# One core, a hybrid decoder layer in three-pass float32: every operand tile of the wide matrix products moved to one start address modulo 512

## The chip, the core and the metric

The kernel runs on one core of a Trainium2 chip. The metric is the device time of one execution in microseconds, the median of several runs. One further execution was recorded by the hardware profiler; every duration below is from that one.

## What is computed

One layer on 16 learned meta tokens and 512 tokens of 1,024 channels. A forgetting-attention branch (8 heads of 128) and an mLSTM branch (4 heads, keys of 256, values of 512, chunks of 128 tokens) read the same normalised input `h`; gates merge them, and one output projection follows. Cut to what matters:

```python
h = rms_norm(x, g_pre)                  # 528 tokens x 1024
z = h @ w_in                            # 1024 x 14352, split into 13 parts
oa = forgetting_attention(fq, fk, fv, log_sigmoid(ff + b_fox_f))
ya = (oa * silu(fz)) @ w_a
qk = silu(causal_conv(mqk, conv_w, conv_b))
hb = sigmoid(mo) * mlstm_scan(mq, mk, mv, ...)
yb = (rms_norm(hb, g_head) * silu(mz)) @ w_b
merged = sigmoid(ga) * ya + sigmoid(gb) * yb
out = x + rms_norm(merged @ w_o, g_post)
```

## The kernel before

Every float32 operand is split into a high part (`..h`, float32r) and a low remainder (`..l`), and each product is made of three passes: high by high, high by low, low by high (`mm3`, lines 132 to 135). One pass is one TensorE instruction with 128 rows and up to 512 moving columns; ahead of each stands a load of its 128 x 128 stationary operand, which the profiler lists as an engine of its own (PEld). While one pass streams its moving operand, the stationary operand of the next is loaded.

Two forms of projection exist. In `proj_t` (line 137) the weights are stationary and 512 tokens of `hh`/`hl` stream; in `proj_wide` (line 160) 128 tokens of `hh`/`hl` are stationary and 512 weight columns stream. For `mo` and `mz` of the mLSTM branch, seven products per block take the place of eight (`st_products`, line 272): their operands are sums of token blocks (`t1` to `t4`, made once by `st_tokens`, line 189) and sums of weight blocks, 256 columns at a time. In `mo` (heads 1 to 3) the token sums are stationary and the weights stream; in `mz` it is the other way round. The order of work per mLSTM head is: transpose and gate the head before, queries and keys with their convolution (264 and 258 columns), `wb` product of the head before (`wb_part`, line 800), values, scores, `mo`, numerator, `mz`. Then come four pairs of attention heads, and last the gates `ga`, the product with `w_a`, and the output projection (`pout`). The instructions of an engine run in program order.

On-chip tiles come from pools. A pool lays its tags behind one another in the order in which they first come up, each as large as the largest tile that asks for it and as often as its `bufs` says, in steps of 64 bytes here; the pools stand behind one another in the order const, wts, work, mlstm, and fox takes the place of mlstm for the second half. 1,152 bytes per partition lie ahead of the first tile. So the start of each tile follows from the sizes, and with it what this text calls the *phase*: the byte address in the partition modulo 512. `hh` and `hl` hold 8 rows (one for each 128 channels) of 528 tokens, 2,112 bytes apart, so that the phase of token 16, where nearly all products begin, moves on by 64 from row to row.

| operand (lines) | phase before | phase after |
|---|---|---|
| `hh`, `hl` from token 16, rows 0 to 7 | 256, 320, 384, 448, 0, 64, 128, 192 | 64 in every row |
| `hm` (meta tokens) | 192 | 64 |
| weight tiles `raw`, `whi`, `wlo`, any block of 128 columns | 256 | 64 |
| `bh`, `bl`, `pth`, `ptl`, `gh1`, `gl1` (tags `big_h`, `big_l`) | 128 | 64 |
| `gh0`, `gl0`, attention values (tags `vh`, `vl`) | 384 | 64 |
| `mh0`, `ml0`; `mh1`, `ml1` (tags `qk0h` to `qk1l`) | 128; 384 and 128 | 64 |
| `mh2`, `ml2`, `mh3`, `ml3` (pool fox) | 320, 64, 320, 320 | 64 |
| token sums `t1` to `t4`, small weight blocks `whs`, `wls` | 320 | 0 |
| attention's meta values `vm` | 256 | 0 |

Of the kernel before, what the change touches and what calls it, by code (L numbers as in the profile page):

```python
# [8 lines left out]
F32 = mybir.dt.float32  # L9
F32R = mybir.dt.float32r  # L10
BF16 = mybir.dt.bfloat16
# [3 lines left out]
P = 128  # L15
DM = 1024
KC = DM // P
SEQ = 512
NM = 16
L = NM + SEQ  # L20
HL = L // 2
NCH = SEQ // P
# [19 lines left out]
OFFA = [0, 144, 416, 816]  # L42
NA = 1344

OFFP = [0, 256, 640, 1152]


@with_exitstack
def tile_hybrid_block(ctx: ExitStack, tc: tile.TileContext, x, meta, norm_pre, norm_post, w_in, b_fox_f,
# [7 lines left out]
    cp = ctx.enter_context(tc.tile_pool(name="const", bufs=1))  # L57
# [6 lines left out]
    def psum1(name):  # L64
        return pa.tile([P, 512], F32, tag="pa", name=name)

    def banks(name, n):

        return [psum1(f"{name}_{i}") for i in range(n)]

    def line(pool, name, n=1, parts=P, **kw):

        return pool.tile([parts, -(-n // 16) * 16], F32, name=name, **kw)[:, 0:n]


    ident = cp.tile([P, P], F32, name="ident")
    make_identity(nc, ident)
    mhalf = line(cp, "mhalf")
    G.memset(mhalf, -0.5)
    hh = cp.tile([P, KC, L], F32R, name="hh")  # L80
    hl = cp.tile([P, KC, L], F32R, name="hl")
    hm = cp.tile([P, KC, P], F32R, name="hm")
    yb = cp.tile([P, KC, SEQ], F32, name="yb")
    gc = cp.tile([P, 96], F32, name="gc")
# [2 lines left out]
    wk = ctx.enter_context(tc.tile_pool(name="work", bufs=1))  # L87
# [1 line left out]
    mw = c1.enter_context(tc.tile_pool(name="mlstm", bufs=1))  # L89

    def sb(shape, dt, tag, name, pool=None, **kw):
        return (pool or wk).tile(shape, dt, tag=tag, name=name, **kw)


    wsrc = sb([P, 512], BF16, "y", "wsrc", bufs=2)
# [20 lines left out]
    def wchunk(*args):  # L116

        return wsplit(wload(*args))
# [13 lines left out]
    def mm3(ps, ah, al, bh, bl, start, stop, **kw):  # L132
        T.matmul(ps, ah, bh, start=start, stop=False, **kw)  # L133
        T.matmul(ps, ah, bl, start=False, stop=False, **kw)  # L134
        T.matmul(ps, al, bh, start=False, stop=stop, **kw)  # L135
# [211 lines left out]
    def stat_part(b):  # L347
        xt, n = xs[b]
        junk = sb([P, 2, 512], BF16, "vh", f"junk{b}")
        ss = line(wk, f"ss{b}", 1, tag="ss", bufs=5)  # L350
        if b == 0:
            half = line(wk, "ss_half", 1, tag="rs", bufs=5)
            junk2 = sb([P, 512], BF16, "y", "junk_half", bufs=2)
            pin(S.activation(junk[:, 0, :], xt[:, 0, :], AF.Square, accum_out=half))
            pin(V.tensor_tensor_reduce(out=junk2, in0=xt[:, 1, :], in1=xt[:, 1, :], op0=ALU.mult, op1=ALU.add,
                                       scale=1.0, scalar=0.0, accum_out=ss))
            pin(V.tensor_tensor(ss, ss, half, ALU.add))
        else:
            pin(S.activation(junk[:n], xt, AF.Square, accum_out=ss[:n]))
        pin(V.tensor_scalar(ss[:n], ss[:n], 1.0 / DM, EPS, ALU.mult, ALU.add))  # L360
        rs = line(wk, f"rs{b}", 1, tag="rs", bufs=5)
        pin(G.tensor_tensor(rs[:n], ss[:n], mhalf[:n], ALU.pow))
        rstd.append(rs)

# [64 lines left out]
    def v_part(h):  # L429
        v = v_tiles(h)  # L430
        w = wchunk(win, 0, KC, C_MV + h * MV, MV, f"wv{h}")
        pn = banks(f"pv{h}", NCH)
        pm = psum1(f"pvm{h}")
        proj_wide(pn, w, pm)
        v_split(*v, pn, pm)
        return v
# [99 lines left out]
    vh, vl, vm = v0  # L536
# [49 lines left out]
    a = gi  # L586
# [137 lines left out]
    def mo_part(h):  # L724
        so = sb([P, NCH, MV], F32, "w", f"so{h}")
        pn = banks(f"po{h}", NCH)

        snaps = [so.rearrange("p s (m n) -> p m s n", m=2)[:, m] for m in range(2)]
        units = [(pn[m], pn[2 + m], snaps[m], slice(m * P, m * P + P)) for m in range(2)]
        st_products(st_wide(C_MO + h * MV, f"wo{h}"), units)  # L730

        dry = line(wk, f"dry{h}", 1, tag="ss", bufs=5)
        pin(S.activation(dry, mhalf, AF.Sigmoid))
        for i in (1, 0):
            for m in range(2):
                dst = so[:, :, i * 256:i * 256 + 256].rearrange("p (s m) n -> p m s n", m=2)[:, m]
                S.activation(dst, units[m][i].rearrange("p (s n) -> p s n", s=2), AF.Sigmoid)
        return so
# [13 lines left out]
    def value_part(h, wpk, v, so, hts, chunks):  # L752
        wh, wl = wpk
        vh, vl, vm = v
        for c in chunks:
            pn = (psum1(f"pna{h}{c}"), psum1(f"pnb{h}{c}"))
            for u in (1, 0):
                o, n = u * 256, 256 + 2 * u
                for j in range(c + 1):
                    s0 = OFF[j] + (c - j) * P  # L760
                    T.matmul(pn[u][:, 0:n], wh[:, s0:s0 + P], vh[:, j, o:o + n], start=(j == 0), stop=False)
                    T.matmul(pn[u][:, 0:256], wh[:, s0:s0 + P], vl[:, j, o:o + 256], start=False, stop=False)
                    T.matmul(pn[u][:, 0:n], wl[:, s0:s0 + P], vh[:, j, o:o + n], start=False, stop=False)
                T.matmul(pn[u][:, 0:n], wh[:, OFFM + c * P:OFFM + (c + 1) * P], vm[:, o:o + n],
                         start=False, stop=True)
            r = line(wk, f"r{h}{c}", 1, tag="r", bufs=4)
            V.tensor_scalar(r, pn[1][:, 256:257], -1.0, col[:, NB + NCH + c, 8 + h:9 + h], ALU.mult, ALU.max)
            V.tensor_tensor(r, pn[1][:, 256:257], r, ALU.max)
            V.reciprocal(r, r)
            if c % 2:  # L770
                ht2 = sb([P, 2, MV], F32, ("qk0h", "qk0l")[c // 2], f"ht{h}{c}")
            ht = ht2[:, c % 2, :]
            for u in range(2):
                V.scalar_tensor_tensor(ht[:, u * 256:u * 256 + 256], pn[u][:, 0:256], r,
                                       so[:, c, u * 256:u * 256 + 256], ALU.mult, ALU.mult)
            junk = sb([P, MV], BF16, "y", f"mjunk{h}{c}", bufs=2)
            ss = line(wk, f"mss{h}{c}", 1, tag="ss", bufs=5)
            S.activation(junk, ht, AF.Square, accum_out=ss)
            V.tensor_scalar(ss, ss, 1.0 / MV, EPS, ALU.mult, ALU.add)
            rs = line(wk, f"mrs{h}{c}", 1, tag="rs", bufs=5)  # L780
            G.tensor_tensor(rs, ss, mhalf, ALU.pow)
            V.tensor_scalar(ht, ht, rs, None, ALU.mult)
            hts[c] = ht
# [37 lines left out]
    for h in range(MH):  # L821
# [6 lines left out]
        if h:  # L828
            w = decay(h)
        if pend is not None:  # L830
            wb_part(pend[0], bt)
        if h == 0:
            v = v0
# [5 lines left out]
            w = decay(0)  # L839
        else:  # L840
            v = v_part(h)
# [74 lines left out]
    def prob_part(p, m, q, k):  # L916
# [7 lines left out]
        for c in range(NCH):  # L924
# [16 lines left out]
            V.reciprocal(rsum, rsum)  # L941
            o = OFFP[c]
            G.tensor_scalar(pn[:, o:o + P].rearrange("p (g t) -> p g t", g=4),  # L943
# [4 lines left out]
    def ptr_part(p, m, pn):  # L948
# [5 lines left out]
        for c in range(NCH):  # L954
            o = OFFP[c]
            pt = psum1(f"pt{h}{c}")
# [45 lines left out]
    q = fq_part(0)  # L1002
    c1.close()
    gp = ctx.enter_context(tc.tile_pool(name="fox", bufs=1))
    go = gp.tile([P, FH, SEQ], F32, tag="go", name="go")
    k = fk_part(0)
    wb_part(MH - 1, bt)
    for p in range(FH // 2):
# [5 lines left out]
        if p % 2 == 0:  # L1014
            v = fv_part(p)
# [46 lines left out]
        S.activation(mh_[u], sa, AF.Copy)  # L1062
        V.tensor_tensor(ml_[u], sa, f(mh_[u]), ALU.subtract)
    og = yb.rearrange("p (b u) t -> p b (u t)", b=NCH)
    oss = line(cp, "oss", NCH * 3).rearrange("p (b i) -> p b i", i=3)
    opre = line(cp, "opre", NCH)

    def out_end(ps, b, c0, n, i):
# [4 lines left out]
    w = wchunk(wo, 0, KC, 0, 512, "wo_0")  # L1073
# [8 lines left out]
    for u in (2, 3):  # L1082
        w = wchunk(wo, 0, KC, u * 256, 256, f"wo{u}")
        for b in range(NCH):
            ps = psum1(f"pout{u}{b}")
            for k in range(KC):
                mm3(ps[:, 0:256], mh_[k // 2][:, k % 2, b * P:(b + 1) * P], ml_[k // 2][:, k % 2, b * P:(b + 1) * P],
                    w[0](k, 0, 256), w[1](k, 0, 256), k == 0, k == KC - 1)
            out_end(ps[:, 0:256], b, u * 256, 256, u - 1)
            if u == 3:  # L1090
                rs = line(wk, f"ors{b}", 1, tag="rs", bufs=5)
                V.scalar_tensor_tensor(rs, oss[:, b, 2:3], 1.0 / DM, opre[:, b:b + 1], ALU.mult, ALU.add)
                G.tensor_tensor(rs, rs, mhalf, ALU.pow)
                for i in range(2):
                    cs = slice(i * 512, i * 512 + 512)
                    V.scalar_tensor_tensor(og[:, b, cs], og[:, b, cs], rs, xr[:, b, cs], ALU.mult, ALU.add)
                    nc.sync.dma_start(out2[b * P:(b + 1) * P, cs], og[:, b, cs])
            elif u == 2:
                V.tensor_reduce(opre[:, b:b + 1], oss[:, b, 0:2], axis=mybir.AxisListType.X, op=ALU.add)
                V.tensor_scalar(opre[:, b:b + 1], opre[:, b:b + 1], 1.0 / DM, EPS, ALU.mult, ALU.add)  # L1100
# [25 lines left out]
```

## Time and profile before

| | |
|---|---|
| median of 3 runs | 958.07 us (957.95 to 959.13) |
| the profiled execution | 959.97 us, of which the span from first to last instruction is 958.1 us |
| TensorE, products (PE) | 942.0 us busy, 98% of the span, 5,720 instructions |
| TensorE, stationary loads (PEld) | 835.7 us busy, 5,720 instructions |
| VectorE, ScalarE, GpSimd | 572.5, 439.7 and 140.4 us busy |
| granted TensorE clock, mean | 0.994 |

In all rows times are microseconds unless a column says ns; L134 is line 134 of the kernel before; `pyb<-bl,wb_h` names what is written and what is read, buffer numbers left out; `128x512` is the moving operand. A matrix product lasts from its start to the end of its last result, and the next one starts long before that, so the durations of neighbours overlap.

### The profile page before, as it was taken

To read this page: it belongs to the slowest core of one execution; us is meant where nothing else is said; L and a number is where in the kernel's file an instruction comes from. 1 tells how busy PE (TensorE), PEld (TensorE's weight loads), DVE (VectorE), ACT (ScalarE), POOL (GpSimd) and SP (SyncE) were. 2 spreads that over 40 slices of the span, in tenths; PEclk is the share of its full clock that TensorE was granted. 3 is DMA by queue.
4 is the path that set the end of the run, shared out by engine and by line. 5 is a ranking of instruction groups with operands and counts; after the bars stand their busy time and mean duration, and the time that the engine had idled before them with its cause. 6 is when DMAs were issued, how large, how long until landed. Compare 5 with 4: busy or idle time off the path is not lost.

```text
span 958.1 us, 14295 instructions
## 1 busy us (share of the span) xinstructions
PE 942.0 (98%) x5720; PEld 835.7 (87%) x5720; DVE 572.5 (60%) x966; ACT 439.7 (46%) x740; POOL 140.4 (15%) x186
## 2 busy tenths in 40 slices
PE   8999899999999999999999999999999999999997
PEld 6998799889998899988999888898888888888887
DVE  6998588448886288862788445445345454444443
ACT  5646446436565255562555224456235365423331
POOL 3054100122001220012112010123111012100000
PEclk9999899999999999999999999999999999999999
DMA  6222143303323223322224242323332322522302
GB/s 225 91 70 78 45 132 97 91 23 93 117 79 102 63 66 111 110 64 80 78 85 164 87 137 68 105 91 111 88 95 95 88 83 72 176 88 92 106 23 89
DMA packets 71469, 90.05 MB, mean 94 GB/s; under 512 B 4965, under 2 KB 56261, under 8 KB 71402
## 3 DMA queue, kind: packets, MB, share of 16 engines
q1 hardware_dynamic: 70344, 89.09, 30.4%
q8 instruction: 45, 0.74, 0.3%
q10 hardware_dynamic: 1058, 0.04, 0.1%
q14 instruction: 22, 0.18, 0.1%
HBM read 86.95 MB, written 2.16 MB: 93 GB/s over the span
## 4 chain that ended last, share of the span: by engine, by line
PE 90%; DVE 4%; ACT 2%; DMA 1%; issue 1%; POOL 1%; POOLq 0%; DVEq 0%; ACTq 0%; SPq 0%
PE pyb L133 3%; PE pyb L135 3%; PE pyb L134 3%; PE pz L134 3%; PE pz L133 3%; PE pz L135 3%; PE pqk L135 3%; PE pqk L133 3%; PE pv L133 3%; PE pv L135 3%; PE pqk L134 3%; PE pv L134 3%; PE po L134 2%; PE po L135 2%; PE po L133 2%; PE pfk L135 2%
## 5 line engine op out<-in xcount | busy, mean ns | idle before, releaser
L943 POOL TENSOR_SCALAR pn<-lt,rsum 128x128 f32<-128x128 f32 x32 | 23.1, 723 | 211.8 <-DVE rsum L941 211.8
L134 PE MATMUL pyb<-bl,wb_h 128*128 128x512 f32 x128 | 50.6, 395 | 0.0
L135 PE MATMUL pyb<-bh,wb_l 128*128 128x512 f32 x128 | 50.6, 395 | 0.0
L133 PE MATMUL pyb<-bh,wb_h 128*128 128x512 f32 x128 | 50.5, 395 | 0.0
L134 PE MATMUL pv<-wv_l,hh 128*128 128x512 f32 (+1 forms) x128 | 46.9, 366 | 1.5 <-DVE wv_l L127 1.5
L135 PE MATMUL pv<-wv_h,hl 128*128 128x512 f32 (+1 forms) x128 | 46.8, 366 | 0.0
L133 PE MATMUL pv<-wv_h,hh 128*128 128x512 f32 (+1 forms) x128 | 46.7, 365 | 0.0
L674 DVE SCALAR_TENSOR_TENSOR y<-z,gc,y 128x512 f32<-128x512 f32 (+1 forms) x48 | 36.0, 754 | 2.2 <-ACT y L667 1.5
L133 PE MATMUL pqk<-hh,wq_h 128*128 128x258 f32 x128 | 36.5, 285 | 0.0
L135 PE MATMUL pfk<-hh,wfk_l 128*128 128x264 f32 x128 | 36.4, 285 | 0.0
L135 PE MATMUL pqk<-hh,wk_l 128*128 128x264 f32 x128 | 36.4, 284 | 0.0
L133 PE MATMUL pfk<-hh,wfk_h 128*128 128x264 f32 x128 | 36.3, 284 | 0.0
L134 PE MATMUL pfk<-hl,wfk_h 128*128 128x264 f32 x128 | 36.3, 284 | 0.0
L133 PE MATMUL pqk<-hh,wk_h 128*128 128x264 f32 x128 | 36.3, 284 | 0.0
L134 PE MATMUL pqk<-hl,wk_h 128*128 128x264 f32 x128 | 36.2, 283 | 0.0
L134 PE MATMUL pqk<-hl,wq_h 128*128 128x258 f32 x128 | 36.1, 282 | 0.0
L135 PE MATMUL pqk<-hh,wq_l 128*128 128x258 f32 x128 | 36.0, 281 | 0.0
L134 PE MATMUL pout<-wo_l,mh 128*128 128x256 f32 (+1 forms) x96 | 30.5, 318 | 0.0
L133 PE MATMUL pout<-wo_h,mh 128*128 128x256 f32 (+1 forms) x96 | 30.5, 317 | 0.0
L135 PE MATMUL pout<-wo_h,ml 128*128 128x256 f32 (+1 forms) x96 | 30.4, 317 | 0.0
L940 ACT ACTIVATE lt<-lt,mn 128x144 f32<-128x144 f32 (+3 forms) x32 | 18.4, 574 | 24.7 <-DVE mn L935 24.6
L134 PEld LDWEIGHTS pv<-wv_l,hh 128*128 128x128 f32 x128 | 24.0, 188 | 6.0 <-DVE wv_l L127 1.7
(979 smaller groups left out, 3297.8 us busy)
## 6 DMA issues: line engine op xcount, KB each, us to landing
wv_r<-in_w_in_dram SPq DMA_DIRECT2D x16, 512.0 KB, 4.4
wo_r<-in_w_in_dram SPq DMA_DIRECT2D x16, 512.0 KB, 4.4
wz_r<-in_w_in_dram SPq DMA_DIRECT2D x16, 512.0 KB, 3.6
wb_r<-in_w_b_dram SPq DMA_DIRECT2D x16, 512.0 KB, 3.5
ab<-d_na SPq DMA_DIRECT2D x8, 672.0 KB, 4.0
wq_r<-in_w_in_dram SPq DMA_DIRECT2D x8, 512.0 KB, 3.8
wk_r<-in_w_in_dram SPq DMA_DIRECT2D x8, 512.0 KB, 3.8
wfq_r<-in_w_in_dram SPq DMA_DIRECT2D x8, 512.0 KB, 3.8
```

The source lines that it names most:

```text
L133: T.matmul(ps, ah, bh, start=start, stop=False, **kw)
L134: T.matmul(ps, ah, bl, start=False, stop=False, **kw)
L135: T.matmul(ps, al, bh, start=False, stop=stop, **kw)
L674: V.scalar_tensor_tensor(y[:, t0:L], z[:, m, t0 + j:L + j], gc[:, j * 16 + mi:j * 16 + mi + 1], y[:, t0:L], ALU.mult, ALU.add)
L940: S.activation(lt[:, 0:kn], lt[:, 0:kn], AF.Exp, bias=mn[:, li:li + 1], scale=-1.0, accum_out=rsum)
L943: G.tensor_scalar(pn[:, o:o + P].rearrange("p (g t) -> p g t", g=4), lt[:, 0:32].unsqueeze(1).to_broadcast([P, 4, 32]), rsum, None, ALU.mult)
```

## The change

No instruction is added or removed. What changes is where the tiles lie:

- `ident` takes 896 bytes in place of 512, and `hh` and `hl` are allocated right behind it, with rows of 640 tokens (2,560 bytes, 5 x 512) of which 528 are used. `mhalf` comes after them.
- `sb`, the helper that allocates all tiles of the pools work, mlstm and fox, now takes a size in bytes from a table by tag (4,096 where the tag is not listed) and cuts the tile that was asked for out of it. The sizes are multiples of 512, apart from the two `y` buffers (2 x 2,304 = 9 x 512).
- The small columns for sums of squares rotate over 8 buffers (tag `ss`) and 7 (tag `rs`) in place of 5 and 5; this moves what lies behind them by 320 bytes.
- `oss`, 64 bytes, moves from the pool const to the front of the pool fox.

Worked out from the sizes this gives the right column of the table above. Keys as stationary operands in `score_part` and `prob_part` and the mLSTM values keep rows of 2,112 bytes, so their phases still vary.

```diff
+BYTES = {"w": 8192, "y": 2304, "vm": 2560, "ptm": 2048, "ab0": 5632, "ab1": 5632, "whs": 2048, "wls": 2048,
+         **{f"qk{i}{x}": 4608 for i in range(2) for x in "hl"}, **{f"v{x}": 8704 for x in "hl"},
+         **{f"big_{x}": 8704 for x in "hl"}}
+
+LP = 640
...
-    ident = cp.tile([P, P], F32, name="ident")
+    ident = cp.tile([P, 224], F32, name="ident")[:, 0:P]
     make_identity(nc, ident)
+    hh = cp.tile([P, KC, LP], F32R, name="hh")[:, :, 0:L]
+    hl = cp.tile([P, KC, LP], F32R, name="hl")[:, :, 0:L]
     mhalf = line(cp, "mhalf")
     G.memset(mhalf, -0.5)
-    hh = cp.tile([P, KC, L], F32R, name="hh")
-    hl = cp.tile([P, KC, L], F32R, name="hl")
...
     def sb(shape, dt, tag, name, pool=None, **kw):
-        return (pool or wk).tile(shape, dt, tag=tag, name=name, **kw)
+
+        n = 1
+        for d in shape[1:]:
+            n *= d
+        size = BYTES.get(tag, 4096)
+        t = (pool or wk).tile([shape[0], size // (2 if dt == BF16 else 4)], dt, tag=tag, name=name, **kw)[:, 0:n]
+        if len(shape) == 3:
+            t = t.rearrange("p (a b) -> p a b", a=shape[1])
+        elif len(shape) == 4:
+            t = t.rearrange("p (a b c) -> p a b c", a=shape[1], b=shape[2])
+        return t
...
-        ss = line(wk, f"ss{b}", 1, tag="ss", bufs=5)
+        ss = line(wk, f"ss{b}", 1, tag="ss", bufs=8)
...
-        rs = line(wk, f"rs{b}", 1, tag="rs", bufs=5)
+        rs = line(wk, f"rs{b}", 1, tag="rs", bufs=7)
...
     gp = ctx.enter_context(tc.tile_pool(name="fox", bufs=1))
+    oss = line(gp, "oss", NCH * 3).rearrange("p (b i) -> p b i", i=3)
...
-    oss = line(cp, "oss", NCH * 3).rearrange("p (b i) -> p b i", i=3)
```

## Rows read from the trace of the kernel before

**Rows 1.** The page, busy time and share of the span by engine.
```profile
PE 942.0 (98%) x5720; PEld 835.7 (87%) x5720; DVE 572.5 (60%) x966; ACT 439.7 (46%) x740; POOL 140.4 (15%) x186
```

**Rows 2.** The page, the chain that ended last, shares of the span by engine.
```profile
PE 90%; DVE 4%; ACT 2%; DMA 1%; issue 1%; POOL 1%; POOLq 0%; DVEq 0%; ACTq 0%; SPq 0%
```

**Rows 3.** Waits of TensorE: total us, times, longest; the longest of nine.
```profile
PE ps L133 <- ACT yb L721: 2.1, 1, 2.1
```

**Rows 4.** The page, granted TensorE clock in 40 slices, tenths of full speed.
```profile
PEclk9999899999999999999999999999999999999999
```

**Rows 5.** TensorE by form, whole run: line, op, out<-in, shapes, count | busy us, mean ns.
```profile
L134 PE MATMUL pyb<-bl,wb_h 128*128 128x512 f32 x128 | 50.6, 395 | 0.0
...
L135 PE MATMUL pv<-wv_h,hl 128*128 128x512 f32 x96 | 37.8, 394 | 0.0
...
L134 PE MATMUL pya<-gl,wa_h 128*128 128x512 f32 x64 | 25.3, 395 | 0.0
...
L135 PE MATMUL pga<-hh,wga_l 128*128 128x512 f32 x64 | 25.2, 393 | 0.0
```

**Rows 6.** Timeline of TensorE, first and last of 96 `pyb` products: start us, us.
```profile
286.42 0.40 PE L133 MATMUL pyb<-bh,wb_h 128*128 128x512 f32 x1
...
308.59 0.39 PE L135 MATMUL pyb<-bh,wb_l 128*128 128x512 f32 x1
```

**Rows 7.** TensorE by form, 942.0 to 943.1 us: `pout`, stationary tiles mh2, mh3.
```profile
L133 PE MATMUL pout<-wo_h,mh 128*128 128x256 f32 x4 | 1.1, 276 | 0.0
```

**Rows 8.** TensorE by form, 943.5 to 944.5 us: `pout`, stationary tiles mh0, mh1.
```profile
L133 PE MATMUL pout<-wo_h,mh 128*128 128x256 f32 x4 | 1.1, 281 | 0.0
```

**Rows 9.** TensorE by form, 823.70 to 824.00 us: `pga`, row 0 of hh.
```profile
L134 PE MATMUL pga<-hl,wga_h 128*128 128x512 f32 x1 | 0.4, 398 | 0.0
L135 PE MATMUL pga<-hh,wga_l 128*128 128x512 f32 x1 | 0.4, 389 | 0.0
L133 PE MATMUL pga<-hh,wga_h 128*128 128x512 f32 x1 | 0.4, 388 | 0.0
```

**Rows 10.** TensorE by form, 824.39 to 824.70 us: `pga`, row 1 of hh.
```profile
L134 PE MATMUL pga<-hl,wga_h 128*128 128x512 f32 x1 | 0.4, 397 | 0.0
L135 PE MATMUL pga<-hh,wga_l 128*128 128x512 f32 x1 | 0.4, 397 | 0.0
L133 PE MATMUL pga<-hh,wga_h 128*128 128x512 f32 x1 | 0.4, 396 | 0.0
```

**Rows 11.** TensorE by form, 517.59 to 517.90 us: `pfq`, row 4 of hh.
```profile
L134 PE MATMUL pfq<-hl,wfq_h 128*128 128x512 f32 x1 | 0.4, 398 | 0.0
L135 PE MATMUL pfq<-hh,wfq_l 128*128 128x512 f32 x1 | 0.4, 389 | 0.0
L133 PE MATMUL pfq<-hh,wfq_h 128*128 128x512 f32 x1 | 0.4, 388 | 0.0
```

**Rows 12.** TensorE by form, 818.30 to 818.42 us: `pga`, row 0, first step of its stage.
```profile
L134 PE MATMUL pga<-hl,wga_h 128*128 128x512 f32 x1 | 0.4, 389 | 0.0
```

**Rows 13.** TensorE by form, whole run: attention output `pfo`, 512 and 256 columns.
```profile
L977 PE MATMUL pfo<-pth,fvh 128*128 128x512 f32 x8 | 3.2, 401 | 0.0
...
L979 PE MATMUL pfo<-pth,fvl 128*128 128x512 f32 x8 | 3.1, 393 | 0.0
...
L978 PE MATMUL pfo<-ptl,fvh 128*128 128x512 f32 x8 | 3.1, 389 | 0.0
...
L977 PE MATMUL pfo<-pth,fvh 128*128 128x256 f32 x8 | 2.3, 284 | 0.0
```

**Rows 14.** TensorE by form, 217.3 to 222.2 us: `mo`, token sums stationary.
```profile
L133 PE MATMUL po<-wo1b_h,t3h 128*128 128x256 f32 x8 | 2.2, 276 | 0.0
```

**Rows 15.** TensorE by form, 115.5 to 117.5 us: `mz`, token sums moving.
```profile
L134 PE MATMUL pz<-t1l,wz00b_h 128*128 128x256 f32 x3 | 0.8, 280 | 0.0
```

**Rows 16.** TensorE by form, whole run: `mo` on plain tokens, and 264 columns.
```profile
L134 PE MATMUL po<-wo1g_l,hh 128*128 128x256 f32 x8 | 2.2, 281 | 0.0
...
L135 PE MATMUL pfk<-hh,wfk_l 128*128 128x264 f32 x128 | 36.4, 285 | 0.0
```

More of the change, by code (lines that the diff above doesn't have):

```diff
@@ L349, in stat_part @@
         junk = sb([P, 2, 512], BF16, "vh", f"junk{b}")
-        ss = line(wk, f"ss{b}", 1, tag="ss", bufs=5)
+        ss = line(wk, f"ss{b}", 1, tag="ss", bufs=8)
         if b == 0:
-            half = line(wk, "ss_half", 1, tag="rs", bufs=5)
+            half = line(wk, "ss_half", 1, tag="rs", bufs=7)
             junk2 = sb([P, 512], BF16, "y", "junk_half", bufs=2)
@@ L730, in mo_part @@
         st_products(st_wide(C_MO + h * MV, f"wo{h}"), units)
-        dry = line(wk, f"dry{h}", 1, tag="ss", bufs=5)
+        dry = line(wk, f"dry{h}", 1, tag="ss", bufs=8)
         pin(S.activation(dry, mhalf, AF.Sigmoid))
@@ L776, in value_part @@
             junk = sb([P, MV], BF16, "y", f"mjunk{h}{c}", bufs=2)
-            ss = line(wk, f"mss{h}{c}", 1, tag="ss", bufs=5)
+            ss = line(wk, f"mss{h}{c}", 1, tag="ss", bufs=8)
             S.activation(junk, ht, AF.Square, accum_out=ss)
             V.tensor_scalar(ss, ss, 1.0 / MV, EPS, ALU.mult, ALU.add)
-            rs = line(wk, f"mrs{h}{c}", 1, tag="rs", bufs=5)
+            rs = line(wk, f"mrs{h}{c}", 1, tag="rs", bufs=7)
             G.tensor_tensor(rs, ss, mhalf, ALU.pow)
@@ L1090, in tile_hybrid_block @@
             if u == 3:
-                rs = line(wk, f"ors{b}", 1, tag="rs", bufs=5)
+                rs = line(wk, f"ors{b}", 1, tag="rs", bufs=7)
                 V.scalar_tensor_tensor(rs, oss[:, b, 2:3], 1.0 / DM, opre[:, b:b + 1], ALU.mult, ALU.add)
```

## The prediction

> **What bounds the kernel now.** I read the page from the top. TensorE's products are busy for 942.0 of 958.1 us [rows 1], the chain that ended last runs through PE for 90% [rows 2], and the longest of TensorE's waits in the whole run is 2.1 us [rows 3]. So the kernel is one long queue of products, and a nanosecond saved on each of them goes straight into the time. The granted clock stands at its upper level, 2.4 GHz, in all slices but the one with the early waits [rows 4]; it is not what this change can move. What is left is how long one product takes, and with that the question becomes whether the address of its operands matters.
>
> The unit needs care. The duration of a product in the rows includes its way through the array, while the next one already streams. What counts is the spacing, start to start. Over 96 `pyb` products the starts go from 286.42 to 308.59 [rows 6], so the spacing is 22.17 / 95 = 233.4 ns; the duration of the same products is 395 ns [rows 5]. The difference, 162 ns, is passed along and not paid, so a duration can be read as spacing plus 162, and a difference of durations is a difference of time.
>
> Does the address matter? The cleanest pair is the end of the kernel: `pout`, the same line, shape, weights and output form, once with `mh2` and `mh3` stationary and once with `mh0` and `mh1`: 276 ns [rows 7] against 281 [rows 8]. Only the place of the stationary tile differs. By the table of phases the weights stream from phase 256; `mh2` and `mh3` lie 64 ahead of that, counted modulo 256, and `mh0` and `mh1` 128. I count modulo 256 because the durations do: row 4 of `hh` starts 256 away from row 0, and its three products have the same 388, 398 and 389 ns [rows 9, 11]. So there is an effect, a few ns in 120 to 230, and what the change does to each family of products depends on the distance between the streaming operand and the stationary one that is loaded meanwhile.
>
> **The change part by part.**
>
> *512 columns, the main term.* By the rows' forms some 2,120 products of 512 columns have both operands in tiles of the table: `pyb` 384, `pv` 288, `pfq`, `pgb`, `pfz` and `pga` 192 each, `pya` and `pfv` 192 each, `po` and `pout` 96 each, the rest 104. Now they lie at all distances and take 393 to 395 ns [rows 5]; I take 394. Afterwards every one has distance 0. The trace has distance 0 in three places, for three products at a time. In `pga`, where the weights lie at 256, row 0 of `hh` gives 388, 398 and 389, mean 391.7 [rows 9]; row 1, with the stream 64 ahead, gives 396.7 [rows 10]. In the first step of the stage the middle product takes 389 as well [rows 12]; with the other two as in rows 9 that is a mean of 388.7. In `pfo`, values and probabilities at 384 and 128, they take 401, 389 and 393, mean 394.3 [rows 13]. A stretch of distance 0 that lasts longer than three products does not occur, and that is the main uncertainty: durations alternate within these steps, so what a long stretch settles to can only be bounded by the three means, 388.7 and 394.3, or by `pyb`, which does settle, at 395. I take 391.7, since it is the step that recurs most (rows 0 and 4 of `hh` in every `proj_t`): 2,120 x 2.3 ns = 4.9 us less. The ends are 2,120 x 5.3 = 11.2 us less, and 2,120 x 1 = 2.1 us more.
>
> *Token sums.* In `mo` the stationary sums lie 64 ahead of the weights: 276 ns [rows 14], 288 products in three heads. Afterwards they lie 64 behind, which is the distance that `mz` has now, 280 ns [rows 15]. In `mz`, 384 products in four heads, the roles are the other way round, and it goes to the distance that `mo` has now. So the two trade places: 288 x 4 = 1.2 us more, 384 x 4 = 1.5 us less, 0.3 us less in all. Here distances are known on both sides.
>
> *Other products of 256 columns.* They go to distance 0, which for 256 columns the trace shows in `pfo` alone, at 284 ns [rows 13]. The 192 of `pout` take 276 and 281 in halves [rows 7, 8], 278.5 on average: 192 x 5.5 = 1.1 us more. Some 504 with plain tokens (`mo` 216, `mz` 192, the second half of head 0's values 96) take 281 [rows 16]: 504 x 3 = 1.5 us more. Should distance 0 be as good as the best row, 276, the 696 would gain 0.5 + 2.5 = 3.0 us. I take the row that has the distance, 2.6 us more.
>
> *264 and 258 columns* (`pqk`, `pfk`, some 1,300). The 264 columns take 285 ns [rows 16] over a mixture of distances; afterwards each row of `hh` has the same distance, 8 to 64. No row here shows one such distance alone. From both sides I allow 2 ns, half the spread between the 276 and 280 of the known distances: 2.6 us either way, and nothing in the sum.
>
> *Everything else* I cost at nothing. The instructions of ScalarE, VectorE and GpSimd stay the same in number and shape, and TensorE's 98% covers VectorE's 60% [rows 1]; a row of 2,560 bytes in place of 2,112 changes only a step. If the cover went, it would be seen as waits above those of rows 3. More buffers for `ss` and `rs` can only loosen waits, and none of TensorE's waits names them. No queue is moved past another, and no wait is added.
>
> *Sum.* 4.9 + 0.3 - 2.6 = 2.6 us less: the profiled execution, 959.97 us, would become 957.4. The median of the runs lies 1.9 us below the profiled execution, so I forecast 955.5 us, 0.27% less.
>
> **The rivals.**
>
> *Distance 0 settles low.* If long stretches do what the first step of the stage does [rows 12], 388.7 ns, the main term is 11.2 us, and the 256 columns are likely to follow with some of their 3.0 us. Sum 11.2 + 0.3 + 0 to 3.0: 944 to 947 us in the median. For it: three products in a row at the lowest durations that occur. Against it: in the same phase relation rows 9 show 398 in the middle, and rows 13 show 401.
>
> *Distance 0 settles high: slower.* `pyb` keeps one distance, 128, for 96 products, and takes 395 ns, more than the 394 of `pv`, which mixes distances. A long stretch can thus lock into a pattern that is worse than the mixture. If distance 0 does so at 395, the main term is 2.1 us more, with 2.6 us from 256 columns and 0.3 us less from the sums: 4.4 us more, 962.5 us. It decides from the point where the settled duration is above 392.9 ns, at which 2,120 x 1.1 us pays for the 256 columns. For it: `pfo`, the one place where six products and more follow at distance 0, is the slowest at 256 columns, 284 ns, and has 394.3 at 512. Against it: the mean of row 0.
>
> *The phase does nothing that adds up.* Distance 0 takes 393 ns at 512 columns and 280 at 256: within 2 us of 958. For it: forms that differ in phase lie within 2 ns of each other over the run [rows 5]. Against it: 276 against 281 in rows 7 and 8. The Trainium skill speaks for this rival on principle: "TensorE: Matmul & The Clock Gate", section "Part 2: What happens when you issue a matmul", gives TensorE two independent read ports and says that loading the next weights does not take read bandwidth from the running matmul, and puts the spacing of warm products of 512 columns at 215.7 ns. By it no address could matter, and the time would stay at 958; the trace does not agree, with 233.4 ns in rows 6 and with rows 7 and 8.
>
> **How the numbers follow.** The forecast, and what lies around it between 950 and 956.1, gets 0.38; settling low 0.14; nothing 0.24; settling high 0.24. About 0.2% of 958, 1.9 us, is what a measurement of this kernel can tell from no change, so faster means below 956.15 and slower above 960.0. Faster is then 0.52, same 0.24, slower 0.24. The range that leaves out 2 in 10 goes from 946.5 (part of settling low stays below) to 962 (a part of settling high, with the 2.6 us of 264 columns on top, above).
>
> **What would show it.** Right: the forms `pyb`, `pya`, `pga`, `pfz` all at the same duration near 391.7, where they were 393 to 395; `mo` with token sums at 280 and `mz` with token sums at 276; `pout` with 256 columns at one duration in both halves, near 284; the other engines unchanged. Wrong: `pyb` at 395 or above (settled high), at 389 or below (settled low), or durations that still vary from row to row of `hh`, which would mean that the distance between the two operands is not what decides. New waits of TensorE would mean that the other engines' times moved with the addresses, which I hold unlikely.

## The result and the profile after

The changed kernel takes 950.3 us (median, 949.6 to 950.8) beside 958.6 us for the kernel before on the same chip: ratio 0.9913, 95% interval 0.9896 to 0.993, 8.3 us less. The profiled execution took 950.76 us with a span of 949.0. The direction was forecast and the time lies in the range, but the forecast saving was 2.6 us and about three times as much came.

The page of the kernel after: busy time of the engines, and the granted clock by slice.

```profile
PE 930.5 (98%) x5720; PEld 835.3 (88%) x5720; DVE 572.7 (60%) x966; ACT 440.0 (46%) x740; POOL 139.4 (15%) x186
...
PEclk9999799999999999999999999999999999999999
```

TensorE's busy time fell by 11.5 us against [rows 1], the span by 9.1; DVE, ACT and POOL did not change in number. One slice of the clock shows 7 where [rows 4] have an 8. Where the 11.5 came from is read in TensorE's groups by form, over the whole run (line, out<-in, shapes, count | busy us, mean ns | idle us before):

```profile
L150 PE MATMUL pyb<-bl,wb_h 128*128 128x512 f32 x128 | 49.8, 389 | 0.0
...
L151 PE MATMUL pv<-wv_h,hl 128*128 128x512 f32 x96 | 37.3, 389 | 0.0
...
L151 PE MATMUL pga<-hh,wga_l 128*128 128x512 f32 x64 | 24.9, 389 | 0.0
...
L150 PE MATMUL pout<-wo_l,mh 128*128 128x256 f32 x64 | 18.1, 283 | 0.0
...
L777 PE MATMUL pnb<-vh,wh 128*128 128x258 f32 x40 | 12.4, 311 | 1.4 <-ACT wh L724 1.4
...
L150 PE MATMUL po<-wo1g_l,hh 128*128 128x256 f32 x8 | 2.3, 283 | 0.0
...
L149 PE MATMUL po<-wo1b_h,t3h 128*128 128x256 f32 x8 | 2.2, 276 | 0.0
```

The lines of code stand 16 further down than in the rows of before. Nearly all forms of 512 columns are at 389 or 390 ns where [rows 5] have 393 to 395; one form each of `pfq`, `pgb` and `po` still averages 393 or 394. `pout` with 256 columns went up to 283 from the 276 and 281 of [rows 7, 8], plain tokens in `mo` from 281 to 283 [rows 16]; `mo` on token sums stayed at the 276 of [rows 14].

What is paid is the spacing of starts. The table adds up, for each family, the time from each product's start to the next one's, in the two profiled executions (products, mean ns of a step before and after, and the difference in us):

| family | products | before | after | us |
|---|---|---|---|---|
| `pyb` | 384 | 233.3 | 227.0 | -2.43 |
| all other 512 columns but `ps` | 1,744 | 232.4 | 227.5 | -8.4 |
| 264 and 258 columns (`pqk`, `pfk`) | 1,152 | 121.0 | 120.4 | -0.75 |
| `mz` on token sums | 384 | 117.9 | 115.0 | -1.11 |
| `mo` on token sums | 288 | 113.3 | 113.3 | 0.00 |
| `pout`, 256 columns | 191 | 116.2 | 120.0 | +0.72 |
| plain tokens, 256 columns (`mo`, `mz`, head 0's `pv`) | 612 | 123.7 | 124.9 | +0.74 |
| `ps` of 128 columns and `pnb` (waits, low clock) | 160 | 148.5 | 161.1 | +2.0 |

These come to -9.2 of the span's -9.1 us. In the last line the kernel after takes longer, and not for its steps alone. TensorE's waits in the kernel after (who waits for whom: us, times, longest):

```profile
PE ps L149 <- ACT yb L737: 3.2, 1, 3.2
...
PE pnb L777 <- ACT wh L724: 1.4, 2, 0.9
```

The wait of [rows 3] grew from 2.1 to 3.2 us, and that of `pnb` from 0.7 to 1.4. TensorE's last product ahead of the longer wait, and ScalarE's work that ends it, first before, then after (timeline):

```profile
98.65 0.27 PE L135 MATMUL ps<-qkh,qkl 128*128 128x128 f32 x1
...
100.24 2.06 ACT L721 ACTIVATE yb<-po 128x512 f32<-128x512 f32 x4
```

```profile
98.50 0.27 PE L151 MATMUL ps<-qkh,qkl 128*128 128x128 f32 x1
...
101.21 2.07 ACT L737 ACTIVATE yb<-po 128x512 f32<-128x512 f32 x4
```

TensorE comes 0.15 us earlier and ScalarE 0.97 us later, so nearly all of the longer wait comes from ScalarE. It does not come from shorter products either: where the weights lie 32 bytes later (below) no family of 512 columns is shorter than before, TensorE's last product starts at 98.83 us, and it waits nearly as long:

```profile
PE ps L151 <- ACT yb L739: 2.7, 1, 2.7
```

Why ScalarE is later in every variant than in the one profiled execution of the kernel before is not shown. Behind the wait the clock differs too. The stretch just behind it, first before, then after (stretch, length, busy us of PE, PEld, DVE, ACT, POOL with counts, granted clock as a share of 2.4 GHz, DMA share, GB/s):

```profile
106.00:108.00 2.00, 1.68 (x11) 1.47 (x12) 1.79 (x5) 0.69 (x3) 0.00 (x0) 0.95 0.01 4
108.00:110.00 2.00, 2.00 (x9) 1.73 (x9) 0.69 (x1) 0.63 (x1) 0.10 (x1) 0.50 0.00 0
110.00:112.00 2.00, 2.00 (x14) 2.00 (x14) 1.51 (x5) 0.17 (x1) 0.00 (x0) 0.70 0.00 0
```

```profile
106.00:108.00 2.00, 1.37 (x4) 0.98 (x5) 1.88 (x6) 1.03 (x3) 0.00 (x0) 0.50 0.00 0
108.00:110.00 2.00, 2.00 (x11) 2.00 (x11) 1.24 (x4) 0.63 (x1) 0.00 (x0) 0.50 0.02 4
110.00:112.00 2.00, 2.00 (x11) 2.00 (x11) 0.84 (x4) 0.00 (x0) 0.10 (x1) 0.50 0.00 0
```

After the longer wait TensorE works at 1.2 GHz (0.50) throughout these six microseconds; before, it had returned to the upper level for part of them. Products of 256 columns, 276 to 283 ns elsewhere, take 415 there, as `pna` did in the kernel before while it ran at 0.50 (count: durations min/median/max, first and last start):

```profile
L777 PE MATMUL pna<-vh,wh x4: 415/415/418, 109.5 to 111.6; 128*128 128x256 f32 x4
```

How long the low clock lasts here does not follow from the products' steps. Over 100 to 114 us the granted clock is 0.76 before and 0.63 after; in two kernels from below that differ, up to there, in no distance between operands (rows of 2,304 bytes, then `out192`) it is 0.63 and 0.76:

```profile
100.00:114.00 14.00, 10.98 (x49) 9.29 (x50) 8.93 (x21) 7.12 (x13) 0.12 (x2) 0.63 0.14 42
```

```profile
100.00:114.00 14.00, 10.74 (x52) 9.12 (x53) 9.08 (x22) 6.85 (x13) 0.48 (x2) 0.76 0.14 38
```

So the 2.0 us of the table's last line are no shown cost of the change: in the other variants, with shorter steps or without, the same 160 products take 0.8 to 2.0 us more than in the execution before.

### The profile page after: what moved, and what is told of

Same layout as the page of the kernel before. It is cut to its first block, busy times and chain, and to the rows that moved or that the text cites. A ratio compares the mean times of both kernels' runs of the same rounds, so it can differ in the third digit from the quotient of the medians.

```text
span 949.0 us, 14296 instructions
## 1 busy us (share of the span) xinstructions
PE 930.5 (98%) x5720; PEld 835.3 (88%) x5720; DVE 572.7 (60%) x966; ACT 440.0 (46%) x740; POOL 139.4 (15%) x186
## 4 chain that ended last, share of the span: by engine, by line
PE 93%; DVE 4%; ACT 1%; issue 1%; DMA 0%; POOL 0%; DVEq 0%; POOLq 0%; ACTq 0%
PE pyb L150 3%; PE pyb L151 3%; PE pyb L149 3%; PE pv L151 3%; PE pv L149 3%; PE pv L150 3%; PE po L149 3%; PE po L150 3%; PE po L151 3%; PE pz L149 3%; PE pz L151 3%; PE pz L150 3%; PE pqk L149 2%; PE pqk L151 2%; PE pqk L150 2%; PE pfk L149 2%
```

## The experiments

All compare with the kernel before, run beside them. "Theory D" is the reading on which the forecast was built, now put to the test: a step depends on the distance, modulo 256 bytes, from the start of a product's stream to the start of the next product's stationary part. "Stationary" weights are those of `pfq`, `pfz`, `pgb`, `pga`, `pyb`, `pya`; in `pv`, `po`, `pfv` and `pout` the weights are the stream.

### The rows back to 2,112 bytes

```
-    hh = cp.tile([P, KC, LP], F32R, name="hh")[:, :, 0:L]
+    hh = cp.tile([P, KC * LP], F32R, name="hh")[:, 0:KC * L].rearrange("p (k t) -> p k t", k=KC)
```

and `hl` alike.

> The token rows of the changed kernel alone go back from 2,560 to 2,112 bytes, with the two tiles kept where they are, so that every other start stays 64 bytes behind a multiple of 512. Theory D (what counts is the distance, modulo 256, from the start of one product's stream to the start of the next product's stationary part): the projections with the tokens meet distances 0, 64, 128 and 192 in turn again, their 512-column products go from about 227 back to about 232 ns a step (some 1,370 products, +6.9 us), their 256-column ones from 120 to 118 (-0.7); the products without tokens (pyb, pya, pout) stay at 227. Time 956 to 958 us. Theory A (each start by itself: a first row at the wanted phase is enough): 950.3, unchanged. Theory N (the gain lies in other things that the change moved, as the token sums or the buffers of small sums): 950.3, with the projections' products still at 227.

Measured: 957.4 us, ratio 0.9989 (0.998 to 0.9998). By form:

```profile
L150 PE MATMUL pyb<-bl,wb_h 128*128 128x512 f32 x128 | 49.9, 390 | 0.0
...
L151 PE MATMUL pv<-wv_h,hl 128*128 128x512 f32 x96 | 37.8, 394 | 0.0
...
L151 PE MATMUL pga<-hh,wga_l 128*128 128x512 f32 x64 | 25.2, 393 | 0.0
```

The products with tokens are back at the 393 and 394 of [rows 5], those without stay at 390. So the row pitch carries some 7 of the 8.3 us, and a good first row is not enough: theory A falls here. One thing was not foreseen: `mo` on token sums, whose own addresses did not move, went from a step of 113.3 to 117.7 ns (+1.3 us). It comes back below.

### Rows of 2,304 bytes: 256 or 512?

```
-LP = 640
+LP = 576
```

> The token rows are 2,304 bytes apart, nine times 256, so that every second row starts 320 bytes behind a multiple of 512 instead of 64; the sizes stay multiples of 512, so that all other starts keep their phase. Theory D (distance modulo 256): nothing changes, 950.3 within 1 us, projections at 227 ns a step. Theory D512 (distance modulo 512, as the change has it): half of the 1,370 512-column products with tokens stand 256 bytes off; if that cost what the other distances cost (some 5 ns) it would give +3.4 us, 953.7.

Measured: 950.3 us, ratio 0.9912 (0.9898 to 0.9927), the same as the changed kernel. The form that meets distances of 0 and 256 in turn:

```profile
L151 PE MATMUL pga<-hh,wga_l 128*128 128x512 f32 x64 | 24.9, 389 | 0.0
```

A multiple of 256 does all that the multiple of 512 does, and needs 4 KB less in each partition.

### The weights alone moved, by 64, 192, 128 and 32 bytes

```
+    cp.tile([P, 16], F32, name="pad_w")
     wk = ctx.enter_context(tc.tile_pool(name="work", bufs=1))
+    wk.tile([P, 112], F32, tag="pad", name="pad")
```

for 64 bytes; the second pad brings all that follows back to its phase. For 192, 128 and 32 the two pads are 48 and 80, 32 and 96, 8 and 120 words.

> The tiles of the weights alone lie 64 bytes later, all others where they were. Theory D: where the weights are stationary (pfq, pfz, pgb, pga, pyb, pya: 1,344 products of 512 columns) the distance becomes +64, and a step goes from 226.8 to the 233.3 ns that pout's split rows at +64 had in the kernel before (+8.7 us); where they are the stream (pv, po, pfv, pout: some 670) it becomes -64, and a step goes to the 229.0 of the kernel before (+1.5). 256 columns: the token sums' products go to 128 (117.9 ns: +1.1 for mz, +1.3 for mo), those at 0 go to 192 or 64 (about -1.8). Time about 961 (959 to 963), slower than the kernel before. Theory A (each start by itself): the weights' start is at fault in both roles alike, all 2,014 products slow down by the same amount; or only the stream's start counts, and then pyb, pya and pga stay at 227.

> The tiles of the weights alone lie 192 bytes later, which is 64 earlier modulo 256: where the weights are stationary the distance is now -64, where they are the stream +64. Theory D with a sign: the two groups change places against the shift by 64: pfq, pfz, pgb, pga, pyb and pya (1,344 products) at about 229.0 ns (+2.6 us), pv, po, pfv and pout's first half (672) at 233.3 (+4.4); mo's and mz's products with token sums at distance 0 and 120.0 (+1.9, +1.9); pout's split part, mo's plain tokens and v's second half leave 120.0 for 113.4 to 117.8 (-1.1 to -3.3). Time 957.8 to 960. Theory R (the role decides: weights 64 off cost 6.5 ns as stationary part and 2.3 as stream, either way): pyb 233.3 and pv 229.0 again, time about 962.

> The tiles of the weights alone lie 128 bytes later. Theory D: the distance is 128 in both roles, so pyb goes from 227 to the 233.3 ns that it had before and the rest to 232.3 to 233.3: 2,014 products by about 6 ns, +12 us; mz t goes from +64 to -64 (+1.1), mo t from -64 to +64 (0), the other 256-column products from 120 to 118 (-1.0). Time about 962 (960 to 964). Theory A: as for a shift by 64, no difference between the two roles and none between 64 and 128 that is known beforehand.

> The tiles of the weights alone lie 32 bytes later, so that the 512-column products stand at a distance of +32 (weights stationary: 1,344) or -32 (weights as the stream: some 670). Theory D-exact (the short step needs the distance 0): they go to 229 to 233.3 ns, as at +64 and -64, and the time to 955 to 961. Theory D-near (starts within 32 bytes count as one place): 227 stays, and 950.3 within 1 us but for the 256-column products, whose places at 32, 96, 160 and 224 no run has shown.

Measured: 961.95 us for 64 (ratio 1.0031, 1.0018 to 1.0044), 958.8 for 192 (1.0007, 0.9998 to 1.0017), 962.8 for 128 (1.0044, 1.003 to 1.0059), 965.4 for 32 (1.0077, 1.0062 to 1.0092). The first three fell where theory D put them (961; 957.8 to 960; 962). The timelines show why: first and last of the 96 `pyb` products that [rows 6] show for the kernel before, and of the 96 of `pout` with 512 columns. The changed kernel:

```profile
286.48 0.39 PE L149 MATMUL pyb<-bh,wb_h 128*128 128x512 f32 x1
...
308.04 0.39 PE L151 MATMUL pyb<-bh,wb_l 128*128 128x512 f32 x1
```

Weights 64 bytes later, then 192 bytes later:

```profile
288.23 0.39 PE L151 MATMUL pyb<-bh,wb_h 128*128 128x512 f32 x1
...
310.39 0.40 PE L153 MATMUL pyb<-bh,wb_l 128*128 128x512 f32 x1
...
910.27 0.39 PE L151 MATMUL pout<-wo_h,mh 128*128 128x512 f32 x1
...
932.02 0.39 PE L153 MATMUL pout<-wo_h,ml 128*128 128x512 f32 x1
```

```profile
287.75 0.39 PE L151 MATMUL pyb<-bh,wb_h 128*128 128x512 f32 x1
...
309.51 0.39 PE L153 MATMUL pyb<-bh,wb_l 128*128 128x512 f32 x1
...
906.49 0.39 PE L151 MATMUL pout<-wo_h,mh 128*128 128x512 f32 x1
...
928.65 0.40 PE L153 MATMUL pout<-wo_h,ml 128*128 128x512 f32 x1
```

Each time over 95 steps: 21.56 us in the changed kernel is 226.9 ns a step. With weights 64 later `pyb` (distance +64) has 233.3 and `pout` (-64) 228.9. With 192, `pyb` (-64) has 229.1 and `pout` (+64) 233.3: the two change places to 0.2 ns, so it is the signed distance and not the role that decides. At 128 `pyb` took 233.4, as in the kernel before, and `pout` 232.3.

The run with 32 bytes was the open one, and it settles that near is not enough: at +32 and at -32 alike, `pyb` and `pout` take 233.3 ns. It lies 4.4 us above the 955 to 961 that were expected if 32 bytes are not near enough, and is the slowest of all: every family of 512 columns stands at 233 ns or more a step, where the shift by 128 leaves several at 232, and `mo` on token sums takes 119.9 ns instead of 113.3 (+1.9 us).

### Everything moved by 64 bytes together

```
-    ident = cp.tile([P, 224], F32, name="ident")[:, 0:P]
+    ident = cp.tile([P, 208], F32, name="ident")[:, 0:P]
```

> Every tile of the changed kernel lies 64 bytes earlier, so that all operands of the 512-column products start at multiples of 512 and the token sums 64 bytes ahead of one; every distance stays what it was. Theory D (distance alone): unchanged, 950.3 within 1 us, the 512-column products at 227 ns a step. Theory A (64 bytes behind a multiple of 512 is a good place by itself): the gain of 8 us is lost in part or whole, up to 958.

Measured: 949.3 us, ratio 0.9909 (0.9895 to 0.9924), which the intervals do not tell from the changed kernel. Every family of 512 columns has the step that it had, to 0.3 ns. So 64 bytes behind a multiple of 512 is nothing special. The 1.4 us by which this span is shorter stand in head 0: from 110 us on the `pna` products ran at the upper clock, those of the changed kernel still at the lower one. The stretch in the form used above:

```profile
110.00:112.00 2.00, 2.00 (x18) 2.00 (x17) 1.25 (x6) 0.00 (x0) 0.10 (x1) 0.94 0.00 0
```

Eighteen products at a clock of 0.94, against eleven at 0.50 in the changed kernel. In the changed kernel the next two microseconds still have 0.67. What makes the clock return about 3 us sooner here, none of these runs tells; the address is not needed for it, as the pair of kernels above shows.

### Token sums at the phase of the rest

```
-            mn = line(wk, f"mn{h}{c}", 2, tag="mn", bufs=4)
+            mn = line(wk, f"mn{h}{c}", 2, tag="mn", bufs=5)
```

and `oss` allocated last in its pool, so that only the token sums and what lies with them move.

> The token sums and what lies with them start 64 bytes behind a multiple of 512 like all else, instead of at multiples of 512. Theory D: mo's and mz's products with token sums come to distance 0, where 256 columns ran at 120.0 ns a step (pout's) instead of 113.3 (mo, 288) and 115.0 (mz, 384): +1.9 and +1.9 us, 954.1 (953 to 955); the 512-column products stay at 227. Theory that the distance is of no account for 256 columns: 950.3.

Measured: 954.06 us, ratio 0.9962 (0.9949 to 0.9975), as theory D had it to 0.1 us.

```profile
L149 PE MATMUL po<-wo1b_h,t3h 128*128 128x256 f32 x8 | 2.3, 283 | 0.0
```

`mo`'s step is 120.0 ns instead of 113.3 (+1.92 us over 288), `mz`'s 120.0 instead of 115.0 (+1.93 over 384). So the part of the change that sets the token sums apart is worth 3.8 us: distance 0, the best place for 512 columns, is among the slowest seen for 256.

### A version for 256 columns, and why it gained nothing

Three of `mo`'s weight tiles, `pout`'s last two weight groups and head 0's second `v` group go 192 bytes later, inside tiles enlarged by 256 bytes, with rows of 2,304:

```
+        t = wp.tile([P, 1088], F32R, tag=tag, name=name)[:, off:off + 1024]
...
-            w = wchunk(wo, 0, KC, u * 256, 256, f"wo{u}")
+            w = wchunk(wo, 0, KC, u * 256, 256, f"wo{u}", off=48)
```

> Token rows 2,304 bytes apart, and of the weights' tiles those that 256-column products stream past the tokens or past mh (pout's last two tiles, mo's three for plain tokens, v's second half in the first head) 192 bytes later, which is a distance of +64. Theory D: 192 products of pout from 120.0 to 113.4 ns (-1.3 us), 216 of mo from 119.9 to 113.4 (-1.4), 96 of v from 120 to 113.4 or 117.8 (-0.2 to -0.6), all 512-column ones at 227: about 947.2 (946.5 to 948.5). Theory that 256 columns settle by how a stretch begins more than by the distance: 950.3 to 949.

Measured: 950.7 us, ratio 0.9924 (0.9907 to 0.994): no gain over the changed kernel, a miss of 3.5 us.

```profile
L154 PE MATMUL pout<-wo_l,mh 128*128 128x256 f32 x64 | 18.0, 281 | 0.0
...
L153 PE MATMUL po<-wo1b_h,t3h 128*128 128x256 f32 x8 | 2.2, 279 | 0.0
```

`pout` went to a step of 117.8 and not to 113.4 (-0.42 us), plain tokens in `mo` to 116.5 (-0.74), and `mo` on token sums, whose distance had not changed, from 113.3 to 117.8 (+1.28). At +64 and at -64 there are thus two steps, 113.3 and 117.8. Both were to be had from the kernel before already: `mo` at +64 had 276 ns [rows 14], `mz` at -64 had 280 [rows 15]. I had taken that as a difference between +64 and -64.

### Two steps at one distance

```
-            w = wchunk(wo, 0, KC, u * 256, 256, f"wo{u}")
+            w = wchunk(wo, 0, KC, u * 256, 256, f"wo{u}", off=16)
```

> As the changed kernel, with token rows of 2,304 bytes, and of the weights' tiles only those of pout's last two groups 64 bytes later: a distance of -64 for its 192 products of 256 columns, nothing else moved. If they settle at 113.3, as in the run with all weights 64 later: 949.0. If they settle at 117.8, as mz's at -64 did in the kernel before: 949.9. If the distance is of no account there: 950.3.

Measured: 949.8 us, ratio 0.9909 (0.9894 to 0.9924). `pout` at -64 stays at 117.8 ns for all 191 steps, although it ran at 113.3 at the same distance where all weights lay 64 later, and `pout` before it had 228.9 instead of 226.9. The same tensors at the same distance, two steps: what differs is what came before.

```
             w = wchunk(wo, 0, KC, u * 256, 256, f"wo{u}", off=48)
...
+            if b == 0:
+                T.matmul(ps[:, 0:64], mh_[0][:, 0, 0:P], w[0](0, 0, 64), start=True, stop=True)
```

> As the changed kernel, with token rows of 2,304 bytes, and pout's last two weight groups 192 bytes later (distance +64, where they ran at 117.8 in the version that also moved mo's), and one extra product of 64 columns ahead of each of the two groups, its result overwritten. If the way in decides which of the two steps seen at +64 a stretch keeps (113.4 or 117.8), the extra product can put it at 113.4: 949.1. If the step belongs to the place, or to the tensors, it stays at 117.8: 949.9 to 950.0.

Measured: 949.75 us, ratio 0.9909 (0.9894 to 0.9924). The products of the first group and, from 931.8 us on, of the second (durations min/median/max, first and last start):

```profile
L154 PE MATMUL pout<-wo_l,mh x28: 276/276/277, 920.5 to 929.7; 128*128 128x256 f32 x28
```

```profile
L154 PE MATMUL pout<-wo_l,mh x22: 281/281/282, 931.9 to 939.3; 128*128 128x256 f32 x22
```

One product of 64 columns let the first group settle at 113.3 ns from its sixth product on, and it stayed there to its end; the second group, with the same extra product but coming from a stretch at 113.3, ran at 117.8. So the way in decides, and a stretch keeps what it has. Which way in leads where is not settled: the extra product did both.

### The version put together

Rows of 2,304 bytes, everything 64 bytes earlier, `pout`'s groups at +64, and the extra product only ahead of the first group (`if u == 2 and b == 0`).

> The version put together from the runs: token rows of 2,304 bytes, all tiles 64 bytes earlier as in the run of that name, pout's last two weight groups at a distance of +64, and one extra product of 64 columns ahead of the first of the two groups alone. If the first group takes the step of 113.4 ns as it did with the extra product, and the second goes on in it because no product stands between them: pout's 192 products give 1.3 us, and from 949.3 to 950.3 the time falls to 948.0 to 949.1. If the second group starts anew at 117.8 or the first doesn't take it: 948.8 to 950.

Measured: 948.9 us (948.45 to 949.4), ratio 0.9903 (0.9886 to 0.9919). The two groups in the same view:

```profile
L154 PE MATMUL pout<-wo_l,mh x29: 276/276/276, 920.4 to 929.9; 128*128 128x256 f32 x29
```

```profile
L154 PE MATMUL pout<-wo_l,mh x23: 276/276/276, 932.0 to 939.5; 128*128 128x256 f32 x23
```

Both groups settle at 113.3 ns; the two together take 1.1 us less than in the changed kernel, the extra product included. Its median is the lowest of all, but its interval overlaps that of the changed kernel. The rest of the span's 2.3 us, 1.2 us, lies ahead of head 0's `mz`, where kernels with the same steps differ too.

## Why the prediction was right and wrong

*What bounds the kernel, and that the distance modulo 256 decides:* right, and now shown for 512 columns: seven runs that moved nothing but addresses fell within 1 us of what the distances gave, one of them on a change of sign. The eighth, by 32 bytes, had no measured step for its distance and came out 4.4 us above its range. That starts of 512 rather than 256 are asked for is more than is needed.

*512 columns, the main term:* the mechanism was right and the size off. 391.7 ns was taken and 389 came; 4.9 us forecast, 10.9 measured. The mean of 398, 389 and 388 in [rows 9] was not the step at which distance 0 settles. The beginning of `pga`'s stage in the changed kernel shows that there is a way into it, with its first eight products and then 42 later ones:

```profile
L150 PE MATMUL pga<-hl,wga_h 128*128 128x512 f32 x3 | 1.2, 393 | 0.0
L149 PE MATMUL pga<-hh,wga_h 128*128 128x512 f32 x3 | 1.2, 392 | 0.0
L151 PE MATMUL pga<-hh,wga_l 128*128 128x512 f32 x2 | 0.8, 389 | 0.0
```

```profile
L151 PE MATMUL pga<-hh,wga_l 128*128 128x512 f32 x14 | 5.4, 389 | 0.0
L149 PE MATMUL pga<-hh,wga_h 128*128 128x512 f32 x14 | 5.4, 389 | 0.0
L150 PE MATMUL pga<-hl,wga_h 128*128 128x512 f32 x14 | 5.4, 389 | 0.0
```

The first five start 229 to 236 ns apart, all that follow 226 or 227. In the kernel before, the distance changed with every third product, so by this reading no row of `hh` at distance 0 ever got past the beginning. `pfo` bears it out: its distance is 0 in both kernels, and its first and third form, 401 and 393 ns in [rows 13], are at 389 after the change:

```profile
L993 PE MATMUL pfo<-pth,fvh 128*128 128x512 f32 x8 | 3.1, 389 | 0.0
...
L995 PE MATMUL pfo<-pth,fvl 128*128 128x512 f32 x8 | 3.1, 389 | 0.0
```

So at 512 columns, too, what a short stretch takes depends on what came before it; only the settled step belongs to the distance. The prediction named what a long stretch settles to as its main uncertainty and had the true value as the lower end, [rows 12] with 388.7, in the rival "distance 0 settles low"; its 512 columns came true, its 256 columns did not. [Rows 9] were chosen because they recur most; but recurring makes a transient no steadier.

*Token sums:* the step "the two trade places" failed. `mo` was to lose 1.2 us and lost nothing, `mz` was to gain 1.5 and gained 1.1. At either sign of 64 both steps occur, and the runs above show that the way in picks one.

*256 columns at distance 0:* right in sign and origin ([rows 13], 284 ns; measured 283). `pout` cost 0.72 us of 1.1 forecast, plain tokens 0.74 of 1.5. `mz` stayed at 118.3 ns: its plain stretches are twelve products long and hardly reach the 120.0 of a long one. Of the 0.74, `mo` has 0.36 and head 0's `pv`, partly through a wait, 0.39.

*264 and 258 columns:* nothing in the sum, 2.6 us allowed either way; 0.75 us less came, over 1,152 products and not some 1,300.

*Everything else at nothing:* in the two profiled executions this was off by 2.0 us: 1.1 us more of waiting ahead of head 0's scores, 0.7 at `pnb`, and a longer stretch at 1.2 GHz. That the change causes it is not shown. The kernels with weights moved by 32, 64 and 128 bytes, whose 512-column steps are no shorter than before in most families, have 0.8 to 1.8 us of it as well, and the clock's part comes and goes between kernels with the same steps. What the prediction left out is how far that place moves by itself; [rows 3] already showed TensorE waiting for ScalarE there, and one profiled execution of the kernel before could not tell.

*The time:* that it fell into the 950 to 956.1 of the forecast is partly luck. By the prediction's own signs, `pyb` at 389 or below is "settled low", for which it gave 944 to 947; the 1.5 us of 256 columns and the 2.0 at head 0 brought the time back to the lower edge of the forecast. `pout` near 284 came as the sign said, `mo` on token sums at 280 did not.

*The rivals:* "settles high" and "the phase does nothing" are out, by 389 ns in nearly every form. "Settles high" leaned on `pfo` as a place where six products and more follow at distance 0; at 512 columns there are three, as the main term says, and the rest are shorter. With the second rival goes what the prediction drew from the Trainium skill ("TensorE: Matmul & The Clock Gate", section "Part 2: What happens when you issue a matmul"): if two independent read ports meant that no address matters, the changed kernel and the runs with moved weights would not differ, and they span 950.3 to 965.4 us; the settled spacing that comes nearest to its 215.7 ns is 226.7.

## What to carry to other kernels

When TensorE is the bound, give the long products' stream and the next stationary part starts that agree modulo 256, rows included, and see that the pitch of a row keeps it so; here that was worth 2 to 3% of every 512-column step. Treat products of another length on their own, for what is best at 512 columns was bad at 256. When a trace shows a setting only for a few products at a time, read it as a beginning, and let its lowest value be an end of the range that deserves a large chance. Before a change of a few us is put down to a wait, look at which of the two engines moved, and whether variants without the change have the wait too.

## What the runs showed of the hardware that was not expected

- Steps of 512-column products by distance: 226.7 to 227.0 ns at 0, 229.0 at -64, 233.3 at +64, 233.3 at +32 and -32, and 232.3 or 233.4 at 128 (`pout` and `pya`, `pyb`). A step that is settled repeats to a tenth of a nanosecond from run to run.
- 256 columns: 120.0 ns at 0, and 113.3 or 117.8 at +64 and -64, kept over 95 to 191 products and changed by one product of 64 columns ahead of the stretch.
- The signed distance counts: exchanging +64 and -64 between the two roles exchanged 233.3 and 229.
- Behind the wait of 3.2 us the granted clock stood at 0.50 for the six microseconds from 106 to 112 us, and 256-column products took 415 ns instead of 276 to 283. Over 100 to 114 us it is 0.63 or 0.76, and kernels with the same steps have either.
- Three products of 512 columns at distance 0 took 401, 389 and 393 ns in `pfo` before the change and 389 each after it, at the same distance.
- Why the distance acts, and what throws a stretch of 256 columns to one step or the other, stays open.
